# Making the low part of split weights with ScalarE and an accumulating DMA instead of a VectorE subtraction

## The chip, the cores and the metric

The kernel runs on one NeuronCore of a Trainium2 chip. The metric is the device time of one execution in microseconds (us). Three executions of the kernel before took 2202.27, 2205.11 and 2205.83 us; the median is 2205.11 us.

A core has five engines with their own instruction queues, each executed in order. TensorE (PE in the profile, PEld for its weight loads) multiplies matrices into PSUM. VectorE (DVE), ScalarE (ACT) and GpSimd (POOL) work elementwise, and SyncE (SP) mostly issues DMA transfers, which 16 DMA engines carry out. Engines wait for each other through semaphores.

## The reference

Two trunk layers of a diffusion backbone with D_MODEL = 1024 run over 128 context tokens and 512 latent tokens, 640 in all. Everything is float32. Cut to what matters, a layer is

```python
h = x * (1 + scale) + shift
z = h @ w_in + b_in                     # 1024 x 11712 weights
out_a .. out_d = four mixers of parts of z    # gated scan, neighbourhood attention, latent attention, convolution
proj = einsum('btnw,nwd->btnd', branches, w_branch)      # four 512 x 1024 weights
mixed = einsum('btnd,btnd->btd', sigmoid(merge gates of z), proj) @ w_out   # 1024 x 1024 weights
y = layer_norm(ALPHA * x + gate * mixed)
```

with `shift`, `scale` and `gate` from a conditioning vector times `w_ada`. The outputs are the tokens of both groups after the last layer and the context states of the mixers.

## The kernel before

Tokens lie along the free dimension, features on the partitions. A large product is done in three passes of a one-pass float32 format (`float32r`): weights and activations are each split as x = hi + lo, and hi·hi, hi·lo and lo·hi are added up in PSUM. Activations are split once per layer. Weights are streamed: a chunk of 128 output columns is loaded, split and used at once.

A chunk goes through `take_w` (L163). SyncE loads the raw float32 weights into `wraw` (three buffers). ScalarE writes the rounded high part into `whi` (L160) and VectorE subtracts it from the raw weights to give `wlo` (L161). `whi` and `wlo` have two buffers each (`NHL = 2`), so the split of a chunk waits until TensorE has finished with the chunk two before it. The raw weights of most chunks are 128 x 1024 elements (512 KB): 184 chunks of `w_in` and 20 of `w_out`. Those of `w_branch` (64 chunks) are 128 x 512 (256 KB). 258 splits go through the `whi` and `wlo` buffers; a few chunks (two of `w_in`, eight of `w_out`) have buffers of their own.

`zchunk` (L242) multiplies one chunk of `w_in`: 48 matmuls at L217, 24 over 384 tokens and 24 over the other 256, in the order hi·h_hi, hi·h_lo, lo·h_hi for each of eight blocks of 128 features. So the third matmul of a chunk is the first that needs `wlo`. `mm3` (L199) does the same for `w_branch` (24 matmuls at L208 for a chunk) and `w_out`. The work of the mixers runs as generators that are advanced one step at a `tick` between halves of chunks, so their matmuls lie between those of the chunks on TensorE.

In the order of the program a layer has these stages: the scan heads with one `w_in` chunk after another; a merge, in which a chunk of `w_in` (merge gate) and a chunk of `w_branch` alternate; latent attention with a second merge; neighbourhood attention with a third; a last merge with no mixer beside it; and the output projection with its norm. At the start, the conditioning products of the first layer are multiplied on TensorE. Later ones (`mod_group`) are products on ScalarE (L382) with sums on GpSimd (L384), beside the scan heads. In neighbourhood attention GpSimd also normalizes the softmax (L880).

The order of instructions on each engine is made by the scheduler of the tile framework; `take_w` raises the priority of its instructions (`W_AHEAD = 300`), so the load and the split of a chunk come early.

Of the kernel before, what the change touches and what calls it, by code (L numbers as in the profile page):

```python
# [13 lines left out]
ALU = mybir.AluOpType  # L14
AX = mybir.AxisListType
PSUM = bass.MemoryType.PSUM
# [10 lines left out]
_OFF = dict(a_q=0, a_ff=512, a_fb=1024, a_i=1536, a_g=2048, b_q=2560, b_k=3072, b_v=3584, b_g=4096,  # L27
            c_qd=4608, c_kvd=4864, c_kpe=4992, c_g=5056, d_b=5568, d_c=6080, d_x=6592, d_g=7104,
            merge=7616)
# [58 lines left out]
class Build:  # L88
# [74 lines left out]
    def take_w(self, src, own=None):  # L163
        with self.tc.high_priority(offset=0 if own in ("s", "t") else self.ahead):
            shape = [128] + [int(x) for x in src.shape[1:]]
            raw = self.wp.tile(shape, F32, name="wraw", tag="wraw", bufs=NRAW)
# [6 lines left out]
            if isinstance(own, tuple):  # L173
                hi, lo = own
            elif own == "s":
                hi, lo = self.s(shape, F32R), self.s(shape, F32R)
            else:
                hi = self.wp.tile(shape, F32R, name="whi", tag="whi", bufs=NHL)
                lo = self.wp.tile(shape, F32R, name="wlo", tag="wlo", bufs=NHL)
            self.split(raw, hi, lo)  # L180
        return hi, lo

    def rsqrt(self, dst, ss, n, scale, eps, mul=None):
        """dst = (ss * scale + eps) ** -0.5 (times mul)"""
# [15 lines left out]
    def mm3(self, outs, w, xs, nk, wsl, xsl):  # L200
        """outs[i] = w.T @ x_i with w = hi + lo, x = hi + lo"""
        nc = self.nc
        hi, lo = w
# [16 lines left out]
    def zopen(self, l, items, own):  # L220
        """chunks whose products start before all of h is there"""
# [15 lines left out]
    def zchunk(self, l, nm, i, ev):  # L237
        """128 columns of the combined projection, transposed; ev takes each part of the tokens from PSUM"""
# [16 lines left out]
    def silu_half(self, l, nm, i, ps, dst):  # L255
        """dst = silu(ps + b)"""
# [19 lines left out]
    def setup(self):  # L276
# [7 lines left out]
        # the scale is kept as 1 + scale  # L284
# [5 lines left out]
        # silu(cond), split, as stationary [hi0 hi1 lo0 lo1]  # L290
# [24 lines left out]
    def setup_late(self):  # L315
        nc, I, cp = self.nc, self.I, self.cp
        # halved, negated (forget gates) and scaled (neighbourhood queries) biases
# [9 lines left out]
        # lower bounds of the forget gates: softmax over depth, cumulated, minus the first  # L327
# [19 lines left out]
    def mod_mm(self, l, g, kb, ps, w):  # L347
        """512 modulation features of both conditions; groups 0-3 hold shift and scale of feature chunks
        2g, 2g+1, groups 4-5 the gates"""
# [5 lines left out]
    def mod_tail(self, l, g, r, ps):  # L355
        """sums of the parts, features on partitions"""
# [15 lines left out]
    def mod_group(self, l, g):  # L372
        """the same away from the start: products with the blocks of the conditions on ScalarE, their sums on
        GpSimd, the sum over the partitions as a product with ones"""
# [62 lines left out]
    def hg_z(self, l, h):  # L437
        nc = self.nc
        G = self.s()      # [g_b | g_f]: products over blocks
        RK = self.s()     # [k_f | k_b]  # L440
        RQ = self.s()     # [q_b | q_f]
# [29 lines left out]
    def hg_mix(self, l, h, z, out):  # L471
# [7 lines left out]
        # v, tokens on partitions  # L479
# [5 lines left out]
        # a token with itself: no decay, both directions  # L485
# [9 lines left out]
        for lev in range(7):  # L495
# [14 lines left out]
            # to blocks of twice the size  # L510
# [10 lines left out]
        # states between the tiles of 128: keys with tokens on partitions, context first  # L521
# [32 lines left out]
        # o, tokens on partitions  # L554
# [23 lines left out]
    def mla_z(self, l):  # L578
# [17 lines left out]
        # kpe twice on the partitions  # L596
# [3 lines left out]
    def rope(self, dst, x):  # L600
        """rotation of the latent columns, two heads on the partitions"""
        nc = self.nc
        for i in range(2):
# [4 lines left out]
            for o in range(4):  # L608
                # halves swapped; the sign is in the table
# [16 lines left out]
    def mla_mix(self, l, z, csg, out):  # L626
# [22 lines left out]
        # latent and cache | context  # L649
# [10 lines left out]
        # rotary keys, shared by the heads, twice on the partitions  # L660
# [13 lines left out]
        for h in range(4):  # L674
            wh, wl, wv = w
            # nope queries (without 1/rms, which goes into the scale of the exponential)
# [9 lines left out]
            # rotary queries, for two heads  # L686
            if h % 2 == 0:
# [9 lines left out]
                # hi and lo of a head stacked, hi where the head lies  # L697
# [8 lines left out]
            # keys: latent and cache | context  # L706
# [11 lines left out]
            # values, tokens on partitions  # L718
# [79 lines left out]
    def softmax(self, sc, n, scale):  # L798
        """rows of exp(scale * (sc - max)) / sum"""
# [13 lines left out]
    def perm_chunk(self, l, nm, c, ctx, lat, bias, scale):  # L813
        """latent tokens from (row, col) to (col, row) order"""
# [13 lines left out]
    def na_z(self, l, c):  # L828
# [4 lines left out]
        # latent and cache | context  # L833
# [8 lines left out]
    # key groups of the latent grid in (col, row) order: start, size  # L842
    KG = ((0, 64), (64, 128), (192, 128), (320, 128), (448, 64))

    def na_mix(self, l, c, z, out):
# [6 lines left out]
        # values, tokens on partitions  # L852
# [11 lines left out]
        # queries: hi and lo of a head stacked, hi where the head lies; keys: hi twice, lo  # L864
# [51 lines left out]
        def TR(j):  # L916
            """keys on partitions, the heads side by side"""
# [74 lines left out]
    def merge_chunk(self, l, n, c, first, last):  # L992
# [10 lines left out]
        for p, (a, e) in enumerate(HALVES):  # L1003
# [9 lines left out]
            if last:  # L1013
                # sigmoid = (1 + tanh) / 2
# [9 lines left out]
    def out_chunk(self, l, c, p, w):  # L1024
        """y = alpha x + gate * (m @ W_out), features on partitions, a part of the tokens"""
# [63 lines left out]
    def out_phase(self, l):  # L1089
        self.y = [None] * 8  # L1090
        self.st = self.cp.tile([128, 5, 8, 6], F32, name="st")
        # the split weights of six chunks stay for the second part of the tokens
# [29 lines left out]
    def h_coef(self, l):  # L1122
        """h = xhat * (g (1 + scale)) + (b (1 + scale) + shift) of layer l + 1; alpha x = xhat * (alpha g) + alpha b"""
# [187 lines left out]
def _bias_index():  # L1311
    """where the entries of the neighbourhood bias lie: rows are queries (col, row) of a tile, columns the
# [86 lines left out]
```

## Time and profile before

| | |
|---|---|
| median of 3 executions | 2205.11 us (2202.27 to 2205.83) |
| span of the profiled execution | 2203.8 us |
| TensorE matmuls busy | 2145.4 us (97% of the span) |
| VectorE busy | 1373.0 us (62%) |
| ScalarE busy | 907.9 us (41%) |
| GpSimd busy | 273.2 us (12%) |
| DMA traffic | 178 MB, 81 GB/s on the mean |

The profile gives the profiled execution its span and no separate device time. The span lies 1.3 us below the median, within the spread of the three executions, so 1.3 us is taken for what lies around it. Busy time is the union of an engine's instructions; TensorE's includes the overlap of pipelined matmuls. `L217` is line 217 of the kernel; names such as `wlo<-wraw,whi` give what an instruction writes and reads. A row "A <- B" of the waits says that A's engine sat idle until B was done.

### The profile page before, as it was taken

The numbers are of one execution on the slowest core, as the hardware profiler recorded it, in microseconds if no ns is written. First come the engines' busy times: TensorE is split into PE (matmuls) and PEld (weight loads), VectorE is DVE, ScalarE is ACT, GpSimd is POOL, SyncE is SP. The second block draws the span as 40 slices with busy tenths as digits, with TensorE's granted clock in tenths as the row PEclk, the third lists the DMA queues.
The fourth block names the chain that finished last, engine by engine and source line by source line (L and its number), as shares of the span: only waits on it lengthen the run. The fifth ranks groups of instructions, "written<-read, shape, count | busy, mean of one in ns | idle before, by whom it ended". The sixth has DMA issues, their size and how long they took to land.

```text
span 2203.8 us, 35726 instructions
## 1 busy us (share of the span) xinstructions
PE 2145.4 (97%) x14538; PEld 2069.4 (94%) x14538; DVE 1373.0 (62%) x2576; ACT 907.9 (41%) x1587; POOL 273.2 (12%) x212
## 2 busy tenths in 40 slices
PE   7899999999999999999999999999999999999997
PEld 4899999999999999999998999999999999989997
DVE  5797878646554556634588877863565535665356
ACT  3445453323333555523355332332333345653332
POOL 0344550000000022200015200000000002121000
PEclk9899999999999999999999999999999999999999
DMA  7323331222112211122432212212221212111241
GB/s 274 109 96 102 119 104 53 61 75 69 61 50 65 66 62 55 58 72 72 144 129 99 82 60 63 65 52 74 64 64 61 65 55 71 59 60 58 72 163 49
DMA packets 70485, 178.06 MB, mean 81 GB/s; under 512 B 7984, under 2 KB 20912, under 8 KB 70320
## 3 DMA queue, kind: packets, MB, share of 16 engines
q1 hardware_dynamic: 67440, 169.32, 23.9%
q10 hardware_dynamic: 2880, 6.45, 0.9%
q8 instruction: 114, 1.87, 0.3%
q14 instruction: 51, 0.42, 0.1%
HBM read 168.20 MB, written 7.54 MB: 80 GB/s over the span
## 4 chain that ended last, share of the span: by engine, by line
PE 85%; DVE 9%; DMA 2%; issue 2%; ACT 2%; POOL 1%; SPq 0%; ACTq 0%; DVEq 0%; POOLq 0%
PE g L217 50%; PE g L208 15%; PE mx L504 2%; PE mx L744 2%; PE mx L958 2%; DVE wlo L161 2%; DMA t<-in_wada 2%; PE mx L906 1%; PE mx L782 1%; PE mx L208 1%; PE mx L905 1%; PE mx L560 1%; PE mx L925 1%; PE mx L217 1%; DVE s L449 1%
## 5 line engine op out<-in xcount | busy, mean ns | idle before, releaser
L217 PE MATMUL g<-h_hi,whi 128*128 128x256 f32 (+1 forms) x2880 | 912.3, 317 | 18.1 <-DVE e L261 7.3
L217 PE MATMUL g<-h_lo,whi 128*128 128x256 f32 (+1 forms) x2880 | 894.3, 311 | 2.6 <-DVE h_lo L409 2.3
L217 PE MATMUL g<-h_hi,wlo 128*128 128x256 f32 (+1 forms) x2880 | 892.9, 310 | 0.6 <-DVE wlo L161 0.6
L217 PEld LDWEIGHTS g<-h_hi,whi 128*128 128x128 f32 x2880 | 549.6, 191 | 31.5 <-DVE e L261 8.9
L217 PEld LDWEIGHTS g<-h_lo,whi 128*128 128x128 f32 x2880 | 550.0, 191 | 4.7 <-DVE h_lo L409 2.9
L217 PEld LDWEIGHTS g<-h_hi,wlo 128*128 128x128 f32 x2880 | 549.7, 191 | 1.0 <-DVE wlo L161 1.0
L161 DVE TENSOR_TENSOR wlo<-wraw,whi 128x1024 fp32r<-128x1024 f32 (+1 forms) x258 | 292.3, 1133 | 320.8 <-ACT whi L160 319.4
L160 ACT CAST whi<-wraw 128x1024 fp32r<-128x1024 f32 (+1 forms) x258 | 242.4, 940 | 450.6 <-PE g L217 252.6
L208 PE MATMUL g<-t,whi 128*128 128x256 f32 (+1 forms) x1280 | 284.2, 311 | 0.0
L880 POOL TENSOR_SCALAR u<-u,sm 128x320 f32<-128x320 f32 (+2 forms) x80 | 89.5, 1130 | 1270.3 <-DVE sm L878 794.5
L208 PEld LDWEIGHTS g<-t,whi 128*128 128x128 f32 x1280 | 214.2, 189 | 2.0 <-ACT s L764 0.8
L384 POOL TENSOR_TENSOR t<-t 128x512 f32<-128x512 f32 x112 | 174.2, 1579 | 273.7 <-ACT t L382 270.9
L208 PE MATMUL g<-t,wlo 128*128 128x384 f32 (+1 forms) x640 | 197.7, 309 | 0.0
L208 PEld LDWEIGHTS g<-t,wlo 128*128 128x128 f32 x640 | 121.1, 189 | 0.0
L996 ACT ACTIVATE e<-g,hbin 128x384 f32<-128x384 f32 (+1 forms) x128 | 67.1, 524 | 128.5 <-PE g L217 128.4
L382 ACT ACTIVATE t<-t,cf 128x512 f32<-128x512 f32 x128 | 90.5, 719 | 71.1 <-DMA t<-in_wada 69.8
L504 PE MATMUL mx<-s,t 128*128 128x128 f32 x560 | 77.4, 286 | 2.7 <-DVE s L516 2.6
L504 PEld LDWEIGHTS mx<-s,t 128*128 128x128 f32 x560 | 73.0, 192 | 3.5 <-ACT e L260 3.1
L260 ACT ACTIVATE e<-g,hbin 128x384 f32<-128x384 f32 x76 | 39.8, 524 | 86.1 <-PE g L217 77.1
L449 DVE RECIPROCAL s<-e 128x384 f32<-128x384 f32 (+1 forms) x32 | 68.7, 2147 | 0.6
L261 DVE TENSOR_SCALAR e<-g,vecs 128x384 f32<-128x384 f32 x76 | 41.1, 541 | 39.9 <-ACT e L260 39.5
L807 ACT ACTIVATE t<-mx,sm,rq 128x640 f32<-128x640 f32 (+1 forms) x40 | 31.9, 797 | 71.9 <-DVE sm L804 68.9
(279 smaller groups left out, 2696.6 us busy)
## 6 DMA issues: line engine op xcount, KB each, us to landing
wraw<-in_win SPq DMA_DIRECT2D x184, 512.0 KB, 3.5
t<-in_wada SPq DMA_DIRECT2D x64, 256.0 KB, 3.9
wraw<-in_wbr SPq DMA_DIRECT2D x64, 256.0 KB, 2.6
wraw<-in_wout SPq DMA_DIRECT2D x20, 512.0 KB, 4.3
s<-in_wada SPq DMA_DIRECT2D x16, 512.0 KB, 7.4
s<-in_nabias SPq DMA_DIRECT2D x8, 640.0 KB, 4.7
m<-in_xT SPq DMA_DIRECT2D x8, 320.0 KB, 8.2
t<-in_xT ACTq DMA_DIRECT2D x8, 320.0 KB, 4.5
```

The lines of the kernel that those rows point to most:

```text
L160: nc.scalar.copy(hi, raw)
L161: nc.vector.tensor_tensor(lo, raw, hi.bitcast(F32), ALU.subtract)
L208: nc.tensor.matmul(o, wsl(a, k), xsl(b, k, i), start=(k == 0 and p == 0), stop=(k == nk - 1 and p == 2))
L217: nc.tensor.matmul(ps[:, :e - a], at(u, k), v[:, k, a:e], start=(k == 0 and i == 0), stop=(k == 7 and i == 2))
L382: nc.scalar.activation(pr[j], raw, AF.Copy, scale=self.cf[:, k, j:j + 1])
L384: nc.gpsimd.tensor_tensor(acc[j], acc[j], pr[j], ALU.add)
L449: nc.vector.reciprocal(g, r)
L504: nc.tensor.matmul(ps[:, j * 128:(j + 1) * 128], km[:, j * 128:(j + 1) * 128], ap_of(RQ, j * 128, [[2 * B, 64 // B], [T + B, 2], [1, B]]), ...
L744: nc.tensor.matmul(ps[:, e * 512:e * 512 + NH], a, b[:, e * NH:(e + 1) * NH], start=(n == 0), stop=(n == 4))
L880: NORM(nc).tensor_scalar(p[e], p[e], sums[:, e:e + 1], None, ALU.mult)
L958: nc.tensor.matmul(o, x[0:sz], y[0:sz, i, :], start=(i == 0 and n == 0), stop=(i == 2 and n == 2))
L996: self.zchunk(l, "merge", n * 8 + c, lambda ps, p, sl: nc.scalar.activation(th[p], ps, AF.Tanh, bias=hb, scale=0.5))
```

## The change

For the chunks in the shared buffers, ScalarE now writes the rounded weights (L181) and then the weights times -1, rounded, into `wlo` (L182). A DMA issued by GpSimd (L183) reads the weights from HBM a second time and adds them onto `wlo`. Chunks with buffers of their own, and all activations, are split as before. Comments are taken out, and lines behind the edit are five further down than before.

```diff
             else:
                 hi = self.wp.tile(shape, F32R, name="whi", tag="whi", bufs=NHL)
                 lo = self.wp.tile(shape, F32R, name="wlo", tag="wlo", bufs=NHL)
+
+                self.nc.scalar.copy(hi, raw)
+                self.nc.scalar.mul(lo, raw, -1.0)
+                self.nc.gpsimd.dma_start(lo, src, accum_op=ALU.add)
+                return hi, lo
             self.split(raw, hi, lo)
         return hi, lo
```

The scheduler moves the new instructions as follows. On ScalarE, in the last merge of the second layer (`e<-g` evicts a merge gate from PSUM, `whi` and `wlo` are weight buffers, wide for `w_in`, narrow for `w_branch`), before:

```order
L996 ACTIVATE e_20349<-g_20357,hbin_532 128x384
L160 CAST whi_20449<-wraw_20447 128x1024
L996 ACTIVATE e_20350<-g_20383,hbin_532 128x256
L160 CAST whi_20507<-wraw_20505 128x512
L996 ACTIVATE e_20445<-g_20453,hbin_532 128x384
```

and now, at the same place:

```order
L1001 ACTIVATE e_20581<-g_20590,hbin_534 128x384
L181 CAST whi_20683<-wraw_20681 128x1024
L182 ACTIVATE wlo_20684<-wraw_20681 128x1024
L1001 ACTIVATE e_20582<-g_20616,hbin_534 128x256
L181 CAST whi_20742<-wraw_20740 128x512
L182 ACTIVATE wlo_20743<-wraw_20740 128x512
L1001 ACTIVATE e_20679<-g_20688,hbin_534 128x384
```

The negated copy stands right behind the rounded copy and ahead of the eviction of the second half. On GpSimd, beside the scan heads of the first layer (L384 and L389 are the sums of the conditioning products), the queue held before only these sums:

```order
L384 TENSOR_TENSOR t_590<-t_590,t_711 128x512
L384 TENSOR_TENSOR t_591<-t_591,t_709 128x512
L384 TENSOR_TENSOR t_590<-t_590,t_762 128x512
L384 TENSOR_TENSOR t_591<-t_591,t_760 128x512
L384 TENSOR_TENSOR t_590<-t_590,t_799 128x512
```

and now:

```order
L389 TENSOR_TENSOR t_593<-t_593,t_715 128x512
L183 DMA wlo_761<-in_win 128x1024
L389 TENSOR_TENSOR t_594<-t_594,t_713 128x512
L389 TENSOR_TENSOR t_593<-t_593,t_767 128x512
L389 TENSOR_TENSOR t_594<-t_594,t_765 128x512
L183 DMA wlo_839<-in_win 128x1024
L183 DMA wlo_938<-in_win 128x1024
L389 TENSOR_TENSOR t_593<-t_593,t_804 128x512
L389 TENSOR_TENSOR t_594<-t_594,t_802 128x512
```

Each of the 258 DMAs waits for its negated copy, and what stands behind it in the queue waits with it; the sums stand ahead of DMAs in turn. The order of the matmuls on TensorE is nearly unchanged behind the start-up.

## The prediction

> **What bounds the kernel now.** I read the page's busy times first, then the groups kept apart by shape, the waits, and the chain of waits in the last merge.
>
> ```profile
> span 2203.8 us, 35726 instructions
> ...
> PE 2145.4 (97%) x14538; PEld 2069.4 (94%) x14538; DVE 1373.0 (62%) x2576; ACT 907.9 (41%) x1587; POOL 273.2 (12%) x212
> ```
>
> TensorE's matmuls cover all but 58 us of the span (2203.8 - 2145.4). Whatever the change does, it can gain at most these 58 us; it loses whatever it puts between two matmuls.
>
> ```profile
> L161 DVE TENSOR_TENSOR wlo<-wraw,whi 128x1024 fp32r<-128x1024 f32 x194 | 248.3, 1280 | 312.2 <-ACT whi L160 311.6
> ...
> L160 ACT CAST whi<-wraw 128x1024 fp32r<-128x1024 f32 x194 | 203.0, 1047 | 367.9 <-PE g L217 243.0 <-PE g L208 59.7 <-issue 39.0
> ...
> L160 ACT CAST whi<-wraw 128x512 fp32r<-128x512 f32 x64 | 39.4, 616 | 82.7 <-PE g L208 58.3 <-issue 14.8 <-PE g L217 9.6
> ```
>
> The splits lie beside that: 194 wide and 64 narrow ones (256 KB of raw weights), a rounded copy on ScalarE (1047 and 616 ns), then a subtraction on VectorE (1280 ns for a wide one).
>
> ```profile
> DVE wlo L161 <- ACT whi L160: 319.4, 124, 7.6
> ...
> ACT whi L160 <- PE g L217: 252.6, 114, 7.3
> ```
>
> VectorE's subtraction waits for the copy, and the copy for TensorE: `whi` and `wlo` have two buffers, so the split of a chunk can start only when the chunk two before it has left TensorE. The split then has the length of one chunk to finish. The chain in the last merge of the first layer shows how long that is.
>
> ```profile
> 1001.49 3.51 PE g L208 x24
> 1005.00 7.03 PE g L217 x48
> ```
>
> A `w_in` chunk (48 matmuls) takes 7.03 us and a `w_branch` chunk (24) 3.51 us, alternating through the stage, 10.55 us for a pair. Nothing but TensorE is on this chain.
>
> ```profile
> 1001.45 1.05 ACT L160 CAST whi<-wraw 128x1024 fp32r<-128x1024 f32 x1 [2.21 <-PE g L217]
> 1002.40 0.47 ACT L996 ACTIVATE e<-g,hbin 128x256 f32<-128x256 f32 x1
> ...
> 1012.00 1.05 ACT L160 CAST whi<-wraw 128x1024 fp32r<-128x1024 f32 x1 [2.21 <-PE g L217]
> ```
>
> The copy for a wide chunk starts at 1001.45, as the wide chunk before it ends, and again at 1012.00. So in this stage a wide chunk's `wlo` has 3.51 us of the narrow chunk between, plus two matmuls of the wide chunk that need no `wlo` (0.35 us: 7.03 / 48 = 0.146 us each on the mean, x 384/320 for the wider half): 3.86 us. The split takes 1.05 and then 1.28 us of it, and 1.5 us are left over. **That margin is what the change spends.**
>
> **Part by part.** *Removed:* 258 subtractions, some 292 us of VectorE. VectorE isn't the bound, but it ends some of TensorE's idle time:
>
> ```profile
> PE g L217 <- DVE e L261: 7.3, 4, 3.3
> ...
> PE mx L573 <- DVE t L568: 0.4, 1, 0.4
> ```
>
> The rows in which VectorE ends TensorE's idle time are 13 (first and last shown) and sum to 36.5 us. Freeing VectorE shortens the others only where a subtraction stood just ahead. I take a third: -12 us, between 0 and -36.
>
> *Added on ScalarE:* 258 negated copies, priced as the rounded copies, whose form they have: 1.05 us wide, 0.62 us narrow, 243 us in all. ScalarE was busy 41%, so the sum is covered, but each lies in line ahead of the DMA. It also stands ahead of the eviction of the second half (1002.40 above) and delays it by 1.05 us; this costs TensorE at most about 0.5 us per pair (the narrow chunk's second half would want that PSUM buffer some 2.1 us after the wide one ends, and it comes at 1.05 + 1.05 + 0.47), and nothing while the next wide chunk waits for longer than that anyway. Not added.
>
> *Added on the DMA:* 258 transfers that read the weights again, read `wlo` and write the sum. The trace has no accumulating DMA and none from GpSimd. Nearest rows:
>
> ```profile
> wraw<-in_win SPq DMA_DIRECT2D x184, 512.0 KB, 3.5
> ...
> wraw<-in_wbr SPq DMA_DIRECT2D x64, 256.0 KB, 2.6
> ...
> s<-in_wada SPq DMA_DIRECT2D x16, 512.0 KB, 7.4
> ```
>
> ```profile
> 1003.79 0.33 SPq L167 DMA_DIRECT2D wraw<-in_wbr  x1
> ```
>
> A plain load lands 3.5 us after its issue for 512 KB and 2.6 us for 256 KB, so 256 KB more cost 0.9 us. Lower bound: a plain load and an issue as short as SyncE's 0.33 us: 3.85 us wide, 2.95 narrow. It can't be less, since the same bytes come from the same place, and something is done to them besides. Upper bound: 512 KB took 7.4 us while all DMA engines were full at the start; with the second operand (2 x 0.9) and the issue 9.6 us, and 6.4 us narrow in proportion. I take 3.5 + 1.8 for the second operand + 0.33 + half of another load's 1.8 us in flight beside it = 6.5 us, and 4.5 us narrow, nearer to the lower end because the DMA engines are busy only 18 to 31% of the time in the stages below.
>
> [...]
>
> So `wlo` of a wide chunk is ready 1.05 + 1.05 + 6.5 = 8.6 us, with 0.2 us allowed for handovers 8.8 us, after its buffer is free; of a narrow one 5.9 us. In the last merge the cover is 3.86 us: TensorE stalls 4.9 us per pair, and the pair takes 15.5 us. Elsewhere the mixers' matmuls lengthen the cover:
>
> ```profile
> 66.00:380.00 314.00, 300.75 (x2105) 298.39 (x2104) 260.50 (x360) 151.26 (x230) 132.76 (x84) 0.98 0.31 101
> 380.00:486.00 106.00, 106.00 (x766) 105.96 (x765) 54.13 (x109) 31.55 (x48) 0.00 (x0) 1.00 0.23 68
> 486.00:640.00 154.00, 153.01 (x1051) 149.07 (x1050) 91.68 (x191) 57.79 (x100) 0.00 (x0) 1.00 0.19 60
> 640.00:860.00 220.00, 218.68 (x1455) 205.95 (x1453) 118.41 (x230) 111.02 (x223) 22.06 (x20) 1.00 0.20 63
> 860.00:945.00 85.00, 85.00 (x545) 77.75 (x546) 54.61 (x116) 43.19 (x99) 22.69 (x20) 1.00 0.18 57
> 945.00:1057.00 112.00, 112.00 (x770) 112.00 (x769) 44.39 (x77) 34.09 (x57) 0.00 (x0) 1.00 0.25 74
> ```
>
> I carried this rule through all chunks behind the start-up, with start and end of each from the times of its matmuls: a chunk starts at its old time plus the delay so far, but not before the end of the chunk two before it plus 8.8 (5.9) us less 0.35. Stalls by stage, layers 0 and 1:
>
> - scan heads (66:380): wide after wide, cover 7.03 us and mixers: 5 and 7 us
> - first merge (380:486): eight pairs with 106 - 8 x 3.51 - 9 x 7.03 = 15 us of mixers among them, so some 2.9 us per pair: 24 and 25 us
> - latent attention and second merge (486:640): 12 and 11 us
> - neighbourhood attention, wide after wide (640:860): 3 and 3 us
> - third merge (860:945): 6 and 4 us
> - last merge (945:1057): ten and eleven pairs: 51 and 53 us
>
> Sum **201 us** in 83 stalls, 40 of them over 1.9 us. At the lower bound it is 63 us (20 such), at the upper 474 us (82).
>
> *The clock.* Long stalls cost a second time:
>
> ```profile
> 322.60:325.90 3.30, 0.02 (x1) 0.00 (x0) 3.16 (x9) 1.35 (x2) 1.37 (x2) 1.00 0.58 178
> 331.50:333.20 1.70, 0.00 (x0) 0.00 (x0) 1.68 (x2) 0.98 (x2) 1.70 (x2) 1.00 0.00 0
> 334.60:338.00 3.40, 3.40 (x17) 3.40 (x17) 3.37 (x5) 0.49 (x1) 0.74 (x1) 0.50 0.27 105
> 659.40:660.70 1.30, 0.01 (x1) 0.01 (x1) 1.24 (x4) 0.00 (x0) 0.00 (x0) 1.00 0.21 19
> 660.70:664.10 3.40, 3.40 (x19) 3.40 (x20) 3.31 (x7) 1.24 (x2) 0.00 (x0) 1.00 0.70 227
> 1229.30:1231.20 1.90, 0.00 (x0) 0.00 (x0) 1.89 (x3) 1.23 (x3) 1.90 (x2) 1.00 0.58 147
> 1232.30:1235.70 3.40, 3.40 (x18) 3.40 (x17) 3.40 (x4) 1.35 (x2) 2.46 (x2) 0.50 0.09 30
> ```
>
> Columns: stretch, its length, busy time of PE, PEld, DVE, ACT and POOL, the granted clock, DMA share, GB/s. A TensorE gap of 3.30 us, and another of 1.76 us behind it, are followed by 3.4 us at half clock; one of 1.9 us alone is too; one of 1.3 us (659.4) is not. So a stall above 1.9 us costs half of 3.4 = 1.7 us more: 40 x 1.7 = **68 us** (20: 34; 82: 139). [...]
>
> *Moved on GpSimd.* A DMA now stands in line with the sums beside the scan heads, and the sums behind it wait with it:
>
> ```profile
> L384 POOL TENSOR_TENSOR t<-t 128x512 f32<-128x512 f32 x112 | 174.2, 1579 | 273.7 <-ACT t L382 270.9 <-ACT e L260 2.6
> ```
>
> GpSimd is busy 132.76 of 314 us there. A DMA that comes at some time meets a running sum in 42% of cases, or a burst; I take half a sum, 0.8 us, for the some 40 chunks that have sums ahead of them. The scan heads have hardly any slack (314 us for 34 chunks are 9.2 us each, less than 9 for most; need 8.8), so this is **+32 us**; nothing where the DMA is as cheap as the lower bound.
>
> **Sum**: 2203.8 + 201 + 68 + 32 - 12 = 2493 us for the profiled execution, and 1.3 us around it: **2494 us**, 13% slower.
>
> **Rivals.** *The DMA is cheap.* At the lower bound 63 + 34 - 12 = +85 us: 2290 us. For it: the DMA engines are mostly idle. Against: second operand.
>
> *The DMA is dear*: a long issue on GpSimd, additions slower than the stream, queueing behind the raw loads. At the upper bound 474 + 139 + 32 - 12 = +633 us: 2838 us, and all stages stall, the scan heads included. For it: nothing of the kind is in the trace, so only the row of the full queues limits it. Against: that row is the worst of the trace.
>
> *GpSimd's queue decides.* If two sums (3.2 us) stand ahead of each of those 40 DMAs, 40 x 3.2 instead of 32 us: 2590 us, with the stalls in the scan heads and not the merges. Against: GpSimd is idle for 58% there.
>
> *Faster.* If copies and DMA together fit in the cover of the last merge, 3.86 us, no stall remains, and the freed VectorE gives up to 36.5 us in the places where TensorE waits for it: 2168 to 2200 us. It decides below a DMA of some 1.6 us; the plain load's 3.5 us speaks against it almost alone.
>
> **How the numbers follow.** Forecast 0.47, cheap 0.18, dear 0.25, GpSimd's queue 0.05, faster or no change 0.05. The forecast's own range, a DMA between 5 and 8 us, is 2385 to 2655 us. The range for 8 in 10 reaches from 2295, just above the cheap end, to 2860, just above the dear end's 2838. A change under 0.2% (4.4 us) can't be told from none in this kernel; the cheap case loses twenty times that. So faster 0.03 and within 0.04 share the last case with a small rest, and slower has 0.93.
>
> **What would show it.** Right: TensorE's gaps ahead of the third matmul of a chunk (`g<-h_hi,wlo`), ended by the `wlo` DMA; a pair in the last merge near 15.5 us; the issue-to-landing of `wlo<-in_win` near 6 us; half-clock windows in all merges; VectorE near 1080 us, ScalarE near 1150 us. Wrong: a pair still near 10.55 us, gaps ended by ScalarE or by VectorE, or stalls that sit in the scan heads while the merges run on. The forecast stands and falls with the one price that the trace doesn't have, the landing time of the accumulating DMA.

## The result: slower by 15.5%, and the profile after

The changed kernel takes 2547.7 us, the median of four executions (2539.84 to 2556.83), against 2204.35 us for the kernel before on the same chip (2202.27 to 2205.83). The ratio is 1.155, with a 95% interval of 1.153 to 1.157. The profiled execution, the slowest of the four, has a span of 2555.0 us, 351 us longer than the 2203.8 us before.

The page of the changed kernel first: busy times, two groups of instructions, and the DMA issues with their size and the median time from issue to landing.

```profile
span 2555.0 us, 36286 instructions
...
PE 2278.5 (89%) x14538; PEld 2156.3 (84%) x14538; DVE 1117.7 (44%) x2318; ACT 1123.0 (44%) x1845; POOL 466.8 (18%) x470
...
L222 PE MATMUL g<-h_hi,wlo 128*128 128x256 f32 (+1 forms) x2880 | 936.5, 327 | 202.4 <-DMA wlo<-in_win 201.8
...
L183 POOL DMA_DIRECT2D wlo<-in_win x182 | 158.3, 870 | 1465.9 <-ACT wlo L182 1388.3
...
wraw<-in_win SPq DMA_DIRECT2D x184, 512.0 KB, 4.0
wlo<-in_win POOLq DMA_DIRECT2D x182, 512.0 KB, 6.8
...
wlo<-in_wbr POOLq DMA_DIRECT2D x64, 256.0 KB, 5.5
```

TensorE issues the same 14538 matmuls, but they now cover 89% of the span instead of 97%. The idle time grew from 58 to 276 us (2555.0 - 2278.5), by 218 us. Of this, 202 us stand ahead of the product with `wlo`, the third matmul of a chunk, and end when the accumulating DMA lands. The plain load of 512 KB lands after 4.0 us, the accumulating one after 6.8 us. VectorE lost 255 us of work and ScalarE gained 215 us; each is busy 44% of the span.

The waits of TensorE say how often, in all, times and the longest:

```profile
PE g L222 <- DMA wlo<-in_win: 201.8, 88, 7.5
PE g L213 <- ACT e L1001: 9.4, 26, 1.2
...
PE g L213 <- DMA wlo<-in_wout: 6.1, 3, 2.8
```

88 waits, 2.3 us each on the mean. One turn of it, in the last merge of the first layer, is in the timeline (start, duration, engine, what, and the idle time before with what ended it):

```profile
1154.98 1.05 ACT L181 CAST whi<-wraw 128x1024 fp32r<-128x1024 f32 x1 [1.97 <-PE g L222]
1155.93 1.06 ACT L182 ACTIVATE wlo<-wraw 128x1024 fp32r<-128x1024 f32 x1
1156.89 0.45 ACT L1001 ACTIVATE e<-g,hbin 128x256 f32<-128x256 f32 x1
...
1157.28 0.86 POOL L183 DMA_DIRECT2D wlo<-in_win  x1 [14.07 <-ACT wlo L182]
1157.40 0.50 PE L213 MATMUL g<-t,whi 128*128 128x256 f32 x2 [0.29 <-ACT e L1001]
...
1159.68 0.39 PE L222 MATMUL g<-h_hi,whi 128*128 128x256 f32 x1 [0.23 <-DVE e L1016]
1159.90 0.28 PE L222 MATMUL g<-h_lo,whi 128*128 128x256 f32 x1
1163.06 0.44 PE L222 MATMUL g<-h_hi,wlo 128*128 128x384 f32 x1 [2.88 <-DMA wlo<-in_win]
1163.34 0.34 PE L222 MATMUL g<-h_hi,whi 128*128 128x384 f32 x1
...
1164.54 0.52 PE L222 MATMUL g<-h_hi,wlo 128*128 128x384 f32 x1
```

The rounded copy starts when the buffer comes free, the negated copy follows, GpSimd takes over 0.3 us later and its issue of the DMA takes 0.86 us. 8.08 us after the start of the copy, TensorE gets its low part and has stood still for 2.88 us. The eviction at 1156.89 stands behind the negated copy, as the order showed, and TensorE waits 0.29 us for it (1157.40).

The rows at 1159.68 and 1159.90 show a change of TensorE's order: two products of the chunk's second half (256 columns) now run ahead of the first product with `wlo`, so four matmuls need no `wlo`, where two did before. The scheduler made this change in 28 of some 180 `w_in` chunks, among them 20 of the 21 in the last merges; behind the start-up the order is therefore not "nearly unchanged" in the stage with the largest stalls. With the two short waits, the cover in this pair is 5.20 us (8.08 - 2.88).

The last row of the fence is the second cost: 1.5 us after the stall a matmul of 384 columns takes 0.52 us instead of 0.34.

The same pair as a row of stretches (length, busy time of PE, PEld, DVE, ACT and POOL, granted clock, DMA share, GB/s), and the half-clock part of it:

```profile
1152.43:1168.77 16.34, 12.94 (x74) 12.09 (x73) 2.76 (x6) 5.04 (x9) 1.73 (x2) 0.90 0.43 96
1163.80:1167.20 3.40, 3.40 (x13) 3.40 (x12) 0.00 (x0) 0.00 (x0) 0.00 (x0) 0.50 0.42 84
```

A pair takes 16.34 us instead of 10.55: 3.40 us without a matmul (16.34 - 12.94), 1.7 us for the 3.4 us at half clock (half of it by the granted clock of 0.50; in it matmuls of 384 columns start 0.32 us apart, behind it 0.18 us), and 0.7 us of further matmul time. The whole span shows what the last may be: TensorE's busy time, with what lies in half-clock windows counted by half, grew by 32 us while its gaps rose from 41 to 184. That is 0.22 us for each gap more, and this pair has three gaps. The clock over the whole span:

```profile
core 0: 2555.0 us, clock 0.946
```

Before it was 0.989. The clock record holds 277.1 us at half clock, before 48.5 us. By the granted clock, half of the difference, 114 us, is the time lost if TensorE was busy throughout; it was busy for 236.6 of these 277.1 us (34.5 of the 48.5 before), so an estimated 101 us of matmul time were lost. So of the 351 us, the waits for the DMA make 208 us (201.8 + 6.1), the clock 101 us, the matmul time that came with the gaps 32 us, and some 10 us are other waits.

By stage, from the start of the first matmul of a chunk to the start of the same matmul of a later chunk, both layers added up (the last merge of layer 1 and all behind it are the last column), in us against the kernel before:

| kernel | start-up | scan heads | first merge | latent attention, 2nd merge | neighb. att. | third merge | last merge and output, layer 0 | the rest |
|---|---|---|---|---|---|---|---|---|
| the change | +1 | +61 | +64 | +41 | +7 | +11 | +86 | +80 |
| third `wlo` buffer (first experiment) | -3 | +27 | +2 | +9 | 0 | 0 | +4 | +4 |
| plain copy (third) | -2 | +20 | +14 | +16 | +2 | 0 | +45 | +34 |
| DMA outside the merges (ninth) | +1 | +69 | +5 | +17 | +10 | 0 | +15 | +8 |
| third buffer, DMA in the merges (tenth) | -3 | +1 | +2 | +3 | 0 | 0 | +2 | +2 |
| ScalarE's second copy unread (twelfth) | -4 | +27 | 0 | +4 | 0 | -2 | 0 | +2 |

### The profile page after: what moved, and what is told of

The parts are those of the page before. It is cut to its first block, busy times and chain, and to the rows that moved or that the text cites. A ratio compares the mean times of both kernels' runs of the same rounds, so it can differ in the third digit from the quotient of the medians.

```text
span 2555.0 us, 36286 instructions
## 1 busy us (share of the span) xinstructions
PE 2278.5 (89%) x14538; PEld 2156.3 (84%) x14538; DVE 1117.7 (44%) x2318; ACT 1123.0 (44%) x1845; POOL 466.8 (18%) x470
## 3 DMA queue, kind: packets, MB, share of 16 engines
q0 software_dynamic: 37152, 118.51, 26.1%
## 5 line engine op out<-in xcount | busy, mean ns | idle before, releaser
L222 PE MATMUL g<-h_hi,wlo 128*128 128x256 f32 (+1 forms) x2880 | 936.5, 327 | 202.4 <-DMA wlo<-in_win 201.8
L222 PE MATMUL g<-h_hi,whi 128*128 128x384 f32 (+1 forms) x2880 | 949.5, 330 | 12.6 <-DVE e L1016 7.8
L222 PE MATMUL g<-h_lo,whi 128*128 128x384 f32 (+1 forms) x2880 | 926.8, 322 | 0.9 <-DVE h_lo L414 0.7
L222 PEld LDWEIGHTS g<-h_hi,wlo 128*128 128x128 f32 x2880 | 576.0, 200 | 230.8 <-DMA wlo<-in_win 230.4
L222 PEld LDWEIGHTS g<-h_hi,whi 128*128 128x128 f32 x2880 | 576.7, 200 | 31.6 <-DVE e L1016 15.3
L181 ACT CAST whi<-wraw 128x1024 fp32r<-128x1024 f32 (+1 forms) x258 | 242.6, 940 | 429.4 <-PE g L222 233.8
L183 POOL DMA_DIRECT2D wlo<-in_win x182 | 158.3, 870 | 1465.9 <-ACT wlo L182 1388.3
L182 ACT ACTIVATE wlo<-wraw 128x1024 fp32r<-128x1024 f32 (+1 forms) x258 | 244.8, 949 | 0.0
L1016 DVE SCALAR_TENSOR_TENSOR e<-e,g 128x384 f32<-128x384 f32 x96 | 46.6, 486 | 315.1 <-PE g L213 314.9
L389 POOL TENSOR_TENSOR t<-t 128x512 f32<-128x512 f32 x112 | 155.8, 1479 | 104.9 <-ACT t L387 104.9
L183 POOL DMA_DIRECT2D wlo<-in_wbr x64 | 55.4, 865 | 247.9 <-ACT wlo L182 240.7
L266 DVE TENSOR_SCALAR e<-g,vecs 128x384 f32<-128x384 f32 x76 | 41.5, 546 | 131.4 <-ACT e L265 131.1
L512 DVE COPY_PREDICATED t<-masks,mx 128x640 f32<-128x640 uint8 x56 | 49.1, 877 | 89.3 <-PE mx L509 89.0
```

Of the source, the lines that this page charges most:

```text
L181: self.nc.scalar.copy(hi, raw)
L182: self.nc.scalar.mul(lo, raw, -1.0)
L183: self.nc.gpsimd.dma_start(lo, src, accum_op=ALU.add)
L222: nc.tensor.matmul(ps[:, :e - a], at(u, k), v[:, k, a:e], start=(k == 0 and i == 0), stop=(k == 7 and i == 2))
L389: nc.gpsimd.tensor_tensor(acc[j], acc[j], pr[j], ALU.add)
L512: nc.vector.copy_predicated(A.rearrange("p (j t) -> p j t", j=5), self.masks[:, lev:lev + 1, :].to_broadcast([128, 5, 128]), ps[:, :T].rea ...
```

## The experiments

The theory: the loss is the latency of copy, copy and DMA beyond the cover that two buffers give, and the half clock that follows. The rivals: the load that the second reads put on the DMA engines, ScalarE's second copy ahead of the evictions, and GpSimd's queue.

**1. A third buffer for the low part.** The DMA keeps its length, but has one chunk more to land in. The negated copy goes first, since its buffer is free earlier; a working slot is given up for room.

```diff
-                lo = self.wp.tile(shape, F32R, name="wlo", tag="wlo", bufs=NHL)
+                lo = self.wp.tile(shape, F32R, name="wlo", tag="wlo", bufs=NHL + 1)
-                self.nc.scalar.copy(hi, raw)
                 self.nc.scalar.mul(lo, raw, -1.0)
+                self.nc.scalar.copy(hi, raw)
-NT_SLOT = 25
+NT_SLOT = 24
```

> The change, but with a third buffer for wlo (one temporary slot of 25 given up for it) and the negated copy issued ahead of the rounded one, so that the low part of a chunk can be made one chunk earlier. Theory (latency): the loss is the time by which the low part, ready some 9.2 us after its buffer is free (1.05 + 1.05 + 0.3 + 6.8), outlasts the one chunk of cover; with two chunks of cover (at least 10.5 us) no stall is left by the rule of the prediction, and the time is 2205 to 2235 us, the rest being the start-up (10 us) and the doubled reads. Rival (DMA load): the second read of 118 MB and the slower raw loads cost time by themselves; then it stays above 2400 us. Rival (ScalarE): the 245 us more on ScalarE cost it; then above 2400 us too.

Measured: 2252.83 us, ratio 1.022 (1.018 to 1.026), above the expected 2205 to 2235 us and far below the rivals' 2400. Its waits and DMA issues:

```profile
PE g L222 <- DMA wlo<-in_win: 4.4, 3, 2.2
```

```profile
wlo<-in_win POOLq DMA_DIRECT2D x182, 512.0 KB, 6.3
...
wlo<-in_wbr POOLq DMA_DIRECT2D x64, 256.0 KB, 4.3
```

The DMA is nearly as long as before (6.3 us), all its bytes are moved and ScalarE does the same work, yet the waits at this place fall from 202 to 4 us, and the stages with a merge lose 2, 9, 0 and 4 us where they lost 64, 41, 11 and 86. So the latency, not the load, made some 295 of the 343 us, with the half clock that it brought. The other 49 us stay, and the next runs ask where they come from.

**2. The low part used last.** The order of the products is changed, in `zmm` (shown) and likewise in `mm3`: in each half of a `w_in` chunk the 16 products with `whi` come first, then the 8 with `wlo`, so the DMA has that much longer.

```diff
-        for k in ks:
-            for i, (u, v) in enumerate(((hi, self.h_hi), (hi, self.h_lo), (lo, self.h_hi))):
...
+        for j, (k, i) in enumerate([(k, i) for k in ks for i in (0, 1)] + [(k, 2) for k in ks]):
+            u, v = ((hi, self.h_hi), (hi, self.h_lo), (lo, self.h_hi))[i]
```

> The change, but within each group of products the ones with the low weights come last: 16 matmuls of a w_in chunk (8 of a w_branch chunk) run before wlo is needed, instead of 2. Theory (latency): the cover of a w_in chunk grows from 0.35 to 2.8 us; the rule of the prediction with the landing times measured since (6.8 and 5.5 us) gives 318 us as is and 132 us here, clock included, so about 2360 us (2330 to 2400). DMA load or ScalarE as the cause: the order of the products changes nothing, 2520 to 2560 us.

Measured: 2318.38 us, ratio 1.051 (1.049 to 1.052). The waits of TensorE for the low part:

```profile
PE g L222 <- DMA wlo<-in_win: 48.6, 36, 3.5
```

They fall from 202 to 49 us without a third buffer, and the time with them. Two buffers still are the limit. It came out better than the expected 2330 to 2400 us.

**3. A plain copy in place of the sum.** GpSimd's DMA writes the weights over the negated ones. The low part is then the weights themselves and the subtraction is left out; queue, bytes read from HBM and ScalarE's work are those of the change.

```diff
-                self.nc.gpsimd.dma_start(lo, src, accum_op=ALU.add)
+                self.nc.gpsimd.dma_start(lo, src)
```

> The change, but the DMA from GpSimd copies the weights into wlo (rounded) instead of adding them: the output lacks the subtraction, the low part is a second high part. Everything waits as before. Term under test: the price of the second operand, 1.8 us of the predicted 6.5. Theory: the landing falls from 6.8 to about 5 us (256 KB: 5.5 to 4.2), and the time by the rule to 2350 to 2420 us. Rival (the way over GpSimd is what is slow, not the adding): the landing stays at 6.2 us or more and the time above 2480 us.

Measured: 2337.16 us, ratio 1.060 (1.057 to 1.062), below the expected 2350 to 2420 us, since the landing fell further than to 5 us. Its DMA issues:

```profile
wraw<-in_win SPq DMA_DIRECT2D x184, 512.0 KB, 3.5
wlo<-in_win POOLq DMA_DIRECT2D x182, 512.0 KB, 4.5
...
wlo<-in_wbr POOLq DMA_DIRECT2D x64, 256.0 KB, 3.9
```

This splits the price: SyncE's load 3.5 us, GpSimd's way 1.0 us more, the sum 2.3 us more again (6.8), for a narrow one 1.6 us (5.5 against 3.9). Each figure counts from the start of the issue, which takes 0.33 us on SyncE, 0.53 us for GpSimd's plain copy and 0.87 us for its accumulating DMA. Shortened by 2.3 us per chunk, the kernel gains 211 us. The scan heads lose 20 us here and 61 us in the change, with the same queue on GpSimd: there too the length of the DMA decides most of it.

**4. ScalarE's work without the second read.** ScalarE writes both copies, and VectorE adds the weights.

```diff
-                self.nc.gpsimd.dma_start(lo, src, accum_op=ALU.add)
+                self.nc.vector.tensor_tensor(lo, raw, lo.bitcast(F32), ALU.add)
```

> ScalarE's part alone: it writes the rounded and the negated copy, and VectorE adds the raw weights onto the negated copy (no second load, no DMA from GpSimd). Theory: ready 1.05 + 1.05 + 1.28 = 3.4 us after the buffer is free, inside the cover of 3.86 us, so 2205 to 2230 us. Rival (ScalarE's extra 245 us and the evictions that wait behind the negated copies are a large part of the loss): above 2300 us.

Measured: 2253.52 us, ratio 1.021 (1.020 to 1.023), a miss: 49 us lost without the second load. In its waits, evictions stand behind the negated copy, as in the change:

```profile
PE g L213 <- ACT e L1001: 9.9, 28, 1.1
PE mx L1054 <- DVE t L1046: 8.0, 3, 5.8
```

28 waits of 0.35 us: the delay that the prediction bounded at 0.5 us per pair and did not add. By stage, the scan heads lose 18 us, latent attention with the second merge 9 us, the last merge and the output phase of layer 0 15 us.

**5. Third buffer, and the negated copy on VectorE.** As the first run, with ScalarE relieved:

```diff
-                self.nc.scalar.mul(lo, raw, -1.0)
+                self.nc.vector.tensor_scalar(lo, raw, -1.0, None, ALU.mult)
```

> As the third-buffer kernel (2253 us), but VectorE writes the negated copy, ScalarE only the rounded one as before the change. Theory: what was left there, 48 us, is ScalarE's doubled work per chunk, as in the kernel with ScalarE's part alone (2254 us, 49 us); without it 2205 to 2225 us. Rival: the doubled reads cost the rest (raw loads and conditioning loads land later); then it stays at 2240 to 2260 us.

Measured: 2247.1 us, ratio 1.019 (1.017 to 1.020), a miss: the 45 us stay with ScalarE back at its old work. Here GpSimd shows up in the waits:

```profile
PE mx L396 <- POOL t L389: 13.9, 5, 6.4
PE g L222 <- DVE e L266: 9.6, 3, 6.5
```

`L389` are the sums of the conditioning products, which now stand behind DMAs in GpSimd's queue; TensorE waits up to 6.4 us for them, against 1.4 us in all before. GpSimd's timeline ahead of the longest of these waits, which ends at 1281.2 us, shows the hold:

```profile
1266.79 6.55 POOL L389 TENSOR_TENSOR t<-t 128x512 f32<-128x512 f32 x5
1278.95 0.88 POOL L183 DMA_DIRECT2D wlo<-in_win  x1 [5.61 <-DVE wlo L181]
1279.56 1.56 POOL L389 TENSOR_TENSOR t<-t 128x512 f32<-128x512 f32 x1
```

After five sums GpSimd stands idle for 5.61 us, because the DMA in line waits for VectorE's negated copy, and the last sum comes behind it. The scan heads lose 31 us.

**6 and 7. The kernel before with one slot less, and with the low part used last.** Each is one edit of the runs above, alone.

> The kernel before with 24 temporary slots instead of 25, the price that the third buffer had. Theory: nothing, 2200 to 2210 us. Rival: the missing slot delays loads and mixers, and some of the 48 us left with the third buffer are its own; then 2220 us or more.

> The kernel before with the products of the low weights last in each group. It says whether the order of the products has an effect of its own. Theory: TensorE waits 0.6 us in all for VectorE's low part, so nothing is to be had, 2198 to 2210 us. Rival: the order itself moves the mixers' steps or the clock and accounts for some of the 230 us won in the changed kernel; then a difference of 10 us or more.

Measured: 2208.69 us for the slot (ratio 1.001, 1.000 to 1.003), some 3 us. And 2229.52 us for the order (1.011, 1.009 to 1.012), a miss: the same work in another order loses 25 us. In its waits two rows stand out:

```profile
PE g L217 <- DVE e L261: 8.3, 3, 7.6
PE mx L504 <- DVE s L516: 7.3, 4, 2.6
```

The longest of these, 7.6 us, lies at 326 us, in the scan heads of layer 0; the scan heads of both layers lose 11 us, the second merge and the output phase 7 us each. The likely reason, not shown by a run, is that the scheduler places the mixers' steps anew around the changed products.

**8. Third buffer, VectorE's negation and the low part last.**

> Third buffer, negated copy by VectorE, and low products last: as much cover for the DMA as there is, and no work added to ScalarE. Theory: no wait for the DMA is left; 2195 to 2220 us, and below the kernel before only if VectorE's freed time (some 100 us of 1373) shortens the waits for it. Rival (doubled reads cost by themselves): 2235 us or more.

Measured: 2252.84 us, ratio 1.021 (1.018 to 1.023), a miss, and no better than the fifth run. More time for the DMA gains nothing once its waits are gone.

**9. The DMA outside the merges only.** The merge gates and `w_branch` are split by VectorE as before; two buffers.

```diff
-    def take_w(self, src, own=None):
+    def take_w(self, src, own=None, acc=True):
...
+                if acc:
+                    self.nc.scalar.copy(hi, raw)
+                    self.nc.scalar.mul(lo, raw, -1.0)
+                    self.nc.gpsimd.dma_start(lo, src, accum_op=ALU.add)
+                    return hi, lo
...
+            w = self.take_w(self.I["win"][l, CC[nm, i]], acc=nm != "merge")
...
+        w = self.take_w(self.I["wbr"][l, n, c], acc=False)
```

> The DMA makes the low part only for the chunks outside the merges (118 of w_in, 12 of w_out); the 64 merge gates and the 64 chunks of w_branch are split by VectorE as before. Two buffers. By the latency theory (a stall is the latency less the cover of the stage) only what the changed kernel loses in the start-up, the scan heads, the neighbourhood attention and the output projection is left: 2265 to 2310 us, with merges at 106 and 113 us as before. If instead every DMA costs the same wherever it stands (343 us for 258 DMAs, 1.33 us each), 130 of them cost 173 us: some 2375 us. What is left beside the waits for the DMA, the third-buffer runs put at some 20 to 30 us in the scan heads.

Measured: 2334.07 us, ratio 1.058 (1.055 to 1.061), 129 us and above the range of 2265 to 2310. The first and third merges are back to +5 and 0 us, near what was expected. What was too low is the rest: the scan heads lose 69 us (61 in the full change), the output projection of layer 0 with the start of the next layer 15 us, and the stages of latent and of neighbourhood attention 17 and 10 us. So half of the DMAs make 38% of the loss. The waits for the DMA alone:

```profile
PE g L223 <- DMA wlo<-in_win: 72.5, 44, 8.1
```

46 of the 72.5 us lie in the scan heads, as in the change (30.1 and 16.2 us there). That is four times what the prediction gave them.

**10. The opposite half, with a third buffer.** The DMA in the merges only, VectorE's subtraction elsewhere; a third `wlo` buffer and one working slot less, as in the first run. `acc` is as in the ninth run, here False unless given.

```diff
-            w = self.take_w(self.I["win"][l, CC[nm, i]])
+            w = self.take_w(self.I["win"][l, CC[nm, i]], acc=nm == "merge")
...
-        w = self.take_w(self.I["wbr"][l, n, c])
+        w = self.take_w(self.I["wbr"][l, n, c], acc=True)
```

> The opposite half, with a third buffer for the low part: the DMA only in the merges (64 merge gates, 64 chunks of w_branch), VectorE's subtraction everywhere else; one working slot less to make room. TensorE's order is now that of the kernel before but for some 220 rows. If the 45 to 49 us that stayed in the runs with a third buffer or with the sum on VectorE come from the order into which the scheduler then puts the scan heads and the output projection, they go: 2205 to 2220 us, scan heads within 2 us of before. If they are a cost of the DMAs or of ScalarE's second copy wherever these stand, about half of them (20 to 25 us) stays: some 2228 us.

Measured: 2215.53 us, ratio 1.005 (1.003 to 1.006), as expected. The largest of TensorE's waits for ScalarE, and the DMA's landing:

```profile
PE g L214 <- ACT e L1002: 5.0, 5, 2.1
```

```profile
wlo<-in_win POOLq DMA_DIRECT2D x64, 512.0 KB, 6.8
```

No wait for the DMA is left, though it takes 6.8 us, and the scan heads are within 1 us of before. So what costs the 45 to 49 us is the change outside the merges, in the scan heads and the output projection, and not its part in the merges. With the slot's 3 us taken off, some 7 us are left for 128 DMAs: hidden, but no gain either.

**11. All the added work, read by nobody.** The kernel before with one slot less; each chunk also gets the negated copy and the accumulating DMA into a scratch tile.

```diff
+                self.split(raw, hi, lo)
+                x = self.wp.tile(shape, F32R, name="scr", tag="scr", bufs=1)
+                self.nc.scalar.mul(x, raw, -1.0)
+                self.nc.gpsimd.dma_start(x, src, accum_op=ALU.add)
+                return hi, lo
```

> The kernel before, its subtraction on VectorE kept, with one working slot less; and beside it for each of the 258 chunks all the added work of the change into a scratch tile that nobody reads: ScalarE's negated copy, and GpSimd's DMA that adds the weights onto it. TensorE's order is that of before but for the start-up and some 90 rows. If the 45 to 49 us that stayed in the runs with a third buffer are the price of that added work (ScalarE's time ahead of evictions, GpSimd's queue, the second reads), they show here too: 2245 to 2260 us. If they come from what waits for the low part and the order into which the scheduler puts it, this kernel loses little more than the slot's 3 us and ScalarE's delay of some evictions: 2208 to 2225 us.

Measured: 2354.41 us, ratio 1.068 (1.064 to 1.071), far above both. The waits of ScalarE say why:

```profile
ACT scr L182 <- DMA wraw<-in_win: 331.7, 114, 7.6
ACT scr L182 <- DMA scr<-in_win: 113.0, 29, 7.7
ACT scr L182 <- DMA scr<-in_wbr: 95.5, 32, 4.6
```

The scratch has one buffer, so ScalarE's next copy waits for the last DMA, and the scheduler put many of these copies ahead of the raw weights' landing.

```profile
PE g L213 <- ACT e L1001: 35.9, 28, 2.2
```

Evictions stand behind the waiting copies and TensorE behind them. The run doesn't answer its question: it adds a wait of its own. It shows what a DMA costs that an instruction in ScalarE's queue waits for.

**12. ScalarE's second copy alone, read by nobody, waiting for nothing.** It reads the rounded weights, so it stands behind the rounded copy; no DMA, and one working slot less.

```diff
+                self.nc.scalar.copy(hi, raw)
+                x = self.wp.tile(shape, F32R, name="scr", tag="scr", bufs=1)
+                self.nc.scalar.mul(x, hi.bitcast(F32), -1.0)
+                self.nc.vector.tensor_tensor(lo, raw, hi.bitcast(F32), ALU.subtract)
+                return hi, lo
```

> As the run with the unread scratch tile, but without the DMA, and with ScalarE's second copy read from the rounded weights, so that it stands behind the rounded copy and waits for nothing else. VectorE's subtraction stays, one working slot less, TensorE's order that of before but for the start-up and some 200 rows. If the 49 us of the run without the second load (ScalarE's two copies, the sum on VectorE) are the price of ScalarE's 243 us in its queue, they show here: 2245 to 2255 us. If they come from the low part being ready one copy later and from the order that the scheduler makes of that, this kernel loses little beside the slot's 3 us: 2207 to 2222 us.

Measured: 2235.08 us, ratio 1.014 (1.012 to 1.016), between the two ranges. The waits of TensorE, and the scan heads of layer 0 as a stretch:

```profile
PE mx L396 <- POOL t L389: 12.1, 11, 2.7
```

```profile
62.40:394.00 331.60, 308.59 (x2103) 304.23 (x2102) 255.61 (x360) 183.68 (x265) 129.27 (x84) 0.96 0.29 96
```

The run loses 31 us, the slot's 3 us included: 27 of them in the scan heads and none in the first, third and last merges. ScalarE also makes the conditioning products there, busy 184 instead of 151 us of the stage; the sums of these products on GpSimd come late, and TensorE waits for them (12.1 us, 1.4 before). So a second copy per chunk is hidden in the merges and is not in the scan heads.

**What stays open.** In the scan heads each part of the change costs something by itself: ScalarE's copies 27 us (twelfth run), the DMAs in GpSimd's queue some of 31 us (fifth), another order of the products 11 us (seventh). They don't add up: all of them together with a third buffer cost 27 us (first). In the first, fifth and twelfth run, 11 us of what the scan heads lose is half clock, and the other 15 to 20 us are gaps of TensorE; so gaps of many causes are paid for twice here as well. How much of each run is the added work, and how much the order into which the scheduler then puts the mixers' steps, the runs don't separate. None of the kernels beats the one before.

## Why the prediction came out as it did

It forecast 2494 us in a range of 2295 to 2860; measured are 2547.7 us. Direction, mechanism and most of the size stand. That the sum came so near is partly luck: in the span, the stalls cost 7 us more than forecast and the clock 33, the 12 us of VectorE did not come, 42 us had no term at all (matmul time at the gaps and other waits), and against this stand 32 us of GpSimd's queue that did not come either. The signs named in the prediction came true, but for the half-clock windows in all merges (the third merge of layer 0 has none). Term by term:

- **Landing of the accumulating DMA**: 6.5 us wide, 4.5 narrow; measured 6.8 and 5.5. The total is near, the parts are not. The 3.5 us of a load already hold SyncE's issue of 0.33 us, which the prediction added once more; GpSimd's way costs 1.0 us over SyncE's, for which it had no term; the second operand costs 2.3 us, where 1.8 us was taken from the step between two loads; and the 0.9 us for another load in flight were not needed to reach the median (3.5 + 1.0 + 2.3 = 6.8).
- **The stalls**: 201 us forecast (the stages as listed add up to 204), 208 measured. By stage the sum hides two errors that cancel, which is luck. The merges and the neighbourhood attention came out near or below the forecast: first merge 19.4 and 21.3 us for 24 and 25, second 11.4 and 11.6 for 12 and 11, third 5.8 and 2.4 for 6 and 4, last 34.6 and 36.9 for 51 and 53. The scan heads came out far above: 30.1 and 16.2 us for 5 and 7, and the start-up and the output phases, which had no stalls in the forecast, hold the other 14 us. The DMA issues of these stretches, medians as on the page: scan heads of layer 0, of layer 1, last merge of layer 0.

```profile
wlo<-in_win POOLq DMA_DIRECT2D x32, 512.0 KB, 8.0
...
wlo<-in_win POOLq DMA_DIRECT2D x33, 512.0 KB, 7.0
...
wlo<-in_win POOLq DMA_DIRECT2D x10, 512.0 KB, 5.8
```

One price was used for all stages, and the scan heads, which have hardly any slack, have the dearest DMA. The stretches show the traffic beside it, a share of 0.61 of the DMA engines, against 0.31 before and 0.42 in the last merge:

```profile
76.60:416.00 339.40, 310.66 (x2091) 301.38 (x2092) 214.51 (x319) 177.94 (x256) 141.87 (x117) 0.97 0.61 142
...
1054.00:1188.00 134.00, 102.59 (x547) 96.16 (x546) 18.58 (x40) 35.14 (x55) 12.92 (x15) 0.85 0.42 94
```

- **The clock**: 68 us forecast, 101 us of matmul time lost (114 by the forecast's count of 1.7 us for a window). With GpSimd's queue this is the largest error of a term. The threshold of 1.9 us was nearly right (of the windows with more than 1.8 us of idle time, 54 of 58 were followed by half clock, below), but the forecast counted one window for each of 40 stalls; there are 49 stalls for the DMA above 1.9 us and 67 more windows than before ((277.1 - 48.5) / 3.41), also in the scan heads and the output phase, and short gaps added up to one in 12 windows of the fourteen traces (below).
- **GpSimd's queue**: +32 us for the scan heads, not borne out as priced. The plain copy has the same queue and loses 20 us there, of which some 8 us are stalls for the DMA and 11 us half clock. A hold exists, with a wait of up to 6.4 us in the fifth run, but what the scan heads of the change lose is stalls for the DMA and half clock.
- **VectorE freed**: -12 us, not seen. VectorE is at 1118 us, near the 1080 forecast, but with the waits for the DMA gone (first run), TensorE's waits for VectorE sum to 41.5 us, no less than the 36.5 before; the largest row is `L266`, 9.9 us.
- **ScalarE's delay of evictions**: not added; 9.4 us in 26 waits (0.36 us each, within the bound of 0.5). What the forecast did not see is ScalarE's copies in the scan heads, where they make the conditioning products late: 27 us in the twelfth run, with the copies alone. "Busy 41%, so the sum is covered" is the step that failed there.
- **The pair of the last merge**: 15.5 us forecast, 16.34 measured, again by errors that cancel. The stall is 2.88 us and not 4.9: the low part is ready after 8.08 us and not 8.8, and the cover is 5.20 us and not 3.86, since four matmuls and two short waits now stand ahead of it and not two matmuls. The half clock (1.7 us, which the forecast added elsewhere), 0.52 us of short waits and 0.7 us of matmul time come on top.

The rivals: *cheap* (2290 us) falls with 6.8 us of landing; *dear* (2838 us) with the same number. *Faster* needed a DMA below 1.6 us; even the plain copy from GpSimd takes 4.5 us. *GpSimd's queue decides* gave 2590 us, near the measured time, but for the wrong reason: it put the stalls in the scan heads and none in the merges, and the merges hold two thirds of them.

## What to carry to other kernels

Before a short operation on an idle engine is replaced by a DMA, compare the latency of the new chain with the cover that the buffers give in the tightest stage, not busy time with busy time: here 2.3 us of copy and subtraction became 9.2 us (1.05 + 1.05 + 0.3 + 6.8, with the median landing; 8.08 us in the pair shown) with 3.9 us of cover (5.2 in that pair), and an engine at 62% had been no reason to relieve it. A third buffer hides such a DMA almost fully (343 us of loss became 49), and then nothing is gained either, since what was relieved was not the bound. In the scan heads, which had hardly any slack, work added on ScalarE, on GpSimd or by another order of the products each cost something, so price an added operation by the busiest stage it runs in.

## What the runs showed of the hardware

In the clock record of the changed kernel all 57 half-clock stretches start at multiples of 3.4133 us from one another, to within 0.002 us; one in the last merge starts at 1163.8 us, the next at 1180.9, five steps on. With the span cut into windows of this length at these starts, and the windows sorted by TensorE's idle time in them: over 1.8 us, 54 of 58 windows were followed by half clock; 1.6 to 1.8 us, 7 of 12; under 1.6 us, 19 of 677. In the kernel before it is 8 of 9 and 3 of 629 for the two ends. Over the windows between the first and the last matmul of all fourteen traces, over 1.8 us were followed by half clock in 217 of 222 cases, under 1.6 us in 117 of 8999; 60 of these 117 windows were themselves at half clock. What brought the half clock in the 117 is not shown. In 12 windows the idle time passed 1.8 us without a single gap of 1.6 us, and all 12 were followed by half clock: there it was the sum of the idle time that stood ahead of it, not one gap. And 4 of the 49 stalls for the DMA above 1.9 us had no half clock behind them; each of the 4 was cut by the end of a window, into parts of at most 1.85 us.

The landing of the accumulating DMA can be split by comparing runs: 3.5 us for 512 KB from SyncE and 1.0 us more from GpSimd, both in the third run, and 2.3 us more for adding, from there to the change. It is not one number: in the change its medians by stage are 5.8 to 8.0 us, in the eleventh run the median is 5.5 us. In the change it is 6.5 us for the 132 wide DMAs of `w_in` with fewer than 1.5 other transfers beside them on the mean, 7.9 us for the 50 with more. With the adding, the DMA engines were also busy for longer. The rows of GpSimd's DMA queue (packets, MB, share of the 16 engines' time), in the change and with the plain copy:

```profile
q0 software_dynamic: 37152, 118.51, 26.1%
...
q0 software_dynamic: 37152, 118.51, 14.8%
```

For the same bytes from HBM that is 26.1% of 2555.0 us against 14.8% of 2331.5 us, 1.93 times the engine time.
